# Queries and keys of layer 1's second eight heads by seven products of halves, all sums made by VectorE

## The chip, the cores and the metric

The kernel runs on one core of one Trainium2 chip. The metric is the time of one execution on the device, in microseconds, taken as the median of several runs.

## The reference

An encoder trunk of two layers on 512 tokens of 1024 channels, in float32. Layer 0 mixes tokens by retention, layer 1 by forgetting attention with 16 heads of 64 channels; every layer norms and modulates its input, and adds a gated branch to it. What matters here is the beginning of layer 1's mixer:

```
q, k, v, g, f = split(h @ w_in, [FOX_W, 2 * FOX_W, 3 * FOX_W, 4 * FOX_W])
q = rms_norm(q per head, q_gain) * 64 ** -0.5
k = rms_norm(k per head, k_gain)
logits = q . k + cum[query] - cum[key], causal, in blocks of 128 queries
o = softmax(logits) . v
y = (o * silu(g)) @ w_out
```

Here h is 512 x 1024, and q, k, v and g are 512 x 1024 each.

## The kernel before

**Precision.** A matmul operand is split into a high part in a shorter format and the rest: ScalarE copies (`CAST`), VectorE subtracts (`split`, line 607). Three matmuls then make one product (`mm3`, line 564): high by high, high by low, low by high. A stationary operand has 128 x 128 elements, a moving one 128 x 512.

**Layer 1's projections.** Heads 0 to 7 are group 0, heads 8 to 15 group 1. For a group, `proj1` (line 1697) makes queries, keys and values one after the other, each 512 tokens by 512 channels. Its weights come as four items of 128 x 1024 (two blocks of 128 input channels by 512 outputs): an item is loaded by SyncE into a buffer `raw`, and split into `wh` and `wl`. `proj_b` (line 1073) multiplies: 4 token tiles x 8 blocks of 128 input channels x 3 matmuls, 96 matmuls per projection, into four PSUM banks `p`. `evac_qk` (line 1529) takes queries and keys out: ScalarE copies the bank to `qn` and squares it into `tm`, VectorE sums the squares per head; after the last token tile VectorE makes the reciprocal roots and scales the four tiles. `evac_v1` (line 1551) splits the values into buffers `v`.

**The heads.** For each pair of heads, `stacks` (line 1566) transposes `qn` and splits it into `st`. For each head, `scores` (line 1590) multiplies queries and keys, VectorE adds `ck` (the running sum of the log forget gates, broadcast by SyncE, with the causal mask added by a POOL DMA) and finds the least, ScalarE makes the exponential, POOL scales by the reciprocal sum; `turn` (line 1626) transposes and splits the probabilities into `ph`; `values` (line 1638) multiplies with `v`. `heads` (line 1668) runs the scores of one head beside the turning of the one before.

**Layer 0's products of halves.** `halves` (line 1092) makes two projections of the same input by a scheme with seven products of half size where the plain way has eight. Tokens, input channels and the two outputs are the halves. It needs four sums of the input's quarters (`sums`), sums of weight blocks, and it adds and subtracts products at the end (`put`). A product is 2 token tiles x 4 blocks of 128 channels x 3 matmuls, 24 matmuls, in two halves `kp` with 12 each; each half has its own `wh` and `wl`. The weight sums are made in place in the `raw` buffers: two of them by VectorE (`sum2`), two by DMAs that add in flight on POOL's queue (`plus`). Layer 0 uses it for values and gates of each head, and for half of the output projection.

**Order of the work.** The program is first built as tasks, and then ordered by a planner, `Sched.order` (line 303). A task's priority is TensorE's planned clock when it is emitted plus an offset: weight splits have -6 us (`PROC`), loads -30, what `merge` (line 493) weaves in as side work -1 (`B1`). Each engine takes the ready task with the lowest value whose buffers are free. The order found is fixed then; on the chip each engine runs its own list in that order, and SyncE and POOL issue their DMAs in theirs.

Near line 1709 the main work of layer 1 stands in this order: queries of group 0 (while `norm_b`, line 1414, norms, transposes and splits the tokens), keys of group 0 with the forget gates woven in, values of group 0 with the first stacks and scores, then queries, keys and values of group 1 with heads 0 to 7 (`R1` = 0.5 of side work per unit of main work), then the gates with heads 8 to 15.

**Buffers.** `KINDS` (line 61) gives each kind of buffer its pool and how many of it may live at a time: pool "C" has 60 buffers of 128 x 512 (`N_C`), pool "B" 14 of 128 x 1024 (`N_B`), shared by `raw` (8), `wh` (4), `wl` (4) and `ck` (3). A buffer is free when the last task that uses it is done.

Of the kernel before, what the change touches and what calls it, by code (L numbers as in the profile page):

```python
# [7 lines left out]
F32R = mybir.dt.float32r  # L8
# [51 lines left out]
START, TICK, TICK_COLS = 0.65, 10.24 / 3, 3072  # L60
KINDS = {
# [470 lines left out]
def trunk(tc, x, c, positions, mod_w, mod_b, norm_g, ret_w_in, ret_w_out, fox_w_in, fox_b_f,  # L532
# [6 lines left out]
    with ExitStack() as es:  # L539
# [337 lines left out]
                spread2()  # L877
        extra = [mod_items(1, "g", j) for j in range(2)]
        for g in range(2):
            for nm_, base in (("q", 0), ("k", 1024), ("v", 2048)):  # L880
                add(("f" + nm_, g), w_b(wi1, base + g * 512))
                while g == 0 and nm_ == "k" and extra:
                    spread()
# [205 lines left out]
                        evac(t, banks[t])  # L1089
                    yield 0.648  # L1090

        def halves(key, src, cols, lows, quarter, sums, put, late=False):

# [65 lines left out]
            if not late:  # L1159
                yield from second()  # L1160
            yield from product(v, lambda: sums[1], sum2(first, 2), True)
            third = plus(block(2), c1, lo)
            u5 = keep(v)
            yield from product(x, lambda: sums[2], sum2(first, 3), False)
            fourth = plus(first, c0, lo)
            u2 = keep(x)
            yield from product(v, lambda: sums[4], heads(block(3)), False)
            put(0, 1, v, u2, ALU.subtract)
# [232 lines left out]
        def norm_a(t):  # L1401
# [9 lines left out]
            for nh in range(2):  # L1411
                V.tensor_scalar(out=xns[t][nh], in0=x1[nh], scalar1=r, scalar2=None, op0=ALU.mult)

        def norm_b(t):
            pss = []
            for hf in range(2):
                ps = pr_()
                for k in range(4):
                    T.transpose(ps[:, k * P:(k + 1) * P], xns[t][hf][:, k * P:(k + 1) * P], ident)
                pss.append(ps)  # L1420
            hvs = [s.buf("xn"), s.buf("xn")]
            for k in range(4):
                for hf in range(2):
                    kk = hf * 4 + k
                    a, b = mod_a[:, 1, kk:kk + 1], mod_s[:, 1, kk:kk + 1]
                    ks = slice(k * P, (k + 1) * P)
                    if hf:
                        V.tensor_scalar(out=hvs[hf][:, ks], in0=pss[hf][:, ks], scalar1=a, scalar2=b,
                                        op0=ALU.mult, op1=ALU.add)
                    else:  # L1430
                        A.activation(hvs[hf][:, ks], pss[hf][:, ks], AF.Identity, scale=a, bias=b)
            ts = slice(t * P, (t + 1) * P)
            for hf in range(2):
                split(hvs[hf].rearrange("p (k n) -> p k n", k=4, n=P), h2t[hf][0][:, :, ts],
                      h2t[hf][1][:, :, ts])
# [93 lines left out]
        def evac_qk(name, g):  # L1529
            qn[name, g] = [None] * NT  # L1530
            ss = small(32)

            def f(t, ps):
                raw, sq = qn_(), tm()
                A.copy(raw, ps)
                A.activation(sq, ps, AF.Square)
                V.tensor_reduce(out=ss[:, t * 8:t * 8 + 8],
                                in_=sq.rearrange("p (h d) -> p h d", h=8, d=HD), axis=AX.X, op=ALU.add)
                qn[name, g][t] = raw
                if t == NT - 1:  # L1540
                    r = rsqrt(ss, 32, 1.0 / HD)
                    for tt in range(NT):
                        v = qn[name, g][tt].rearrange("p (h d) -> p h d", h=8, d=HD)
                        rr = r[:, tt * 8:tt * 8 + 8]
                        V.tensor_tensor(out=v, in0=v, in1=rr.unsqueeze(2).to_broadcast([P, 8, HD]),
                                        op=ALU.mult)
            return f

        vt = {}

# [146 lines left out]
        def proj1(names, g, lead=0):  # L1697
            for name in names:
                ev = evac_v1(g) if name == "v" else evac_qk(name, g)
                yield from proj_b(lambda i: W(("f" + name, g), i), h2, ev, lead=lead)  # L1700
# [6 lines left out]
                norm_b(t + 2)  # L1707
        run(q0)
        merge(proj1("k", 0), forget_gates(), 0.5, B1, s)
        merge(proj1("v", 0), chain(stacks(0), stacks(1), scores(0)), 0.3, B1, s)  # L1710
        merge(proj1("qkv", 1), heads(0, 8, 16), R1, B1, s)
        merge(chain(*[proj_g(j) for j in range(4)]), heads(8, 16, 16), R2, B1, s)


# [87 lines left out]
```

## Time and profile before

| what | before |
|---|---|
| median of 3 runs | 717.82 us (715.70 to 718.38) |
| the profiled execution | 717.73 us, span 716.0 us |
| mean granted TensorE clock | 0.996 |
| TensorE busy | 704.0 us, 3388 matmuls |
| VectorE busy | 593.0 us, 1233 instructions |
| ScalarE busy | 409.9 us, 765 instructions |
| GpSimd busy | 119.3 us, 171 instructions |
| bytes moved by DMA | 120.37 MB, of these 111.25 MB read from HBM |

A row of a group names the line, engine and operation, then output <- inputs by the program's buffer names, the shape, the count, and after the bars the busy time in us and the mean of one in ns, and the engine's idle time before it. Nearly every instruction has line 452, where the planned tasks are sent, so groups are told apart by their buffers. A row of the windows has start and end in us from the span's start, the length, the busy time of each engine with its instructions, the granted clock, and the DMA engines' share and rate. PE is TensorE's matmul, PEld its weight load, DVE VectorE, ACT ScalarE, POOL GpSimd, SP SyncE.

### The profile page before, as it was taken

How to read it: one execution, taken by the hardware profiler on the slowest of the kernel's cores; microseconds unless marked ns; L12 is line 12 of the kernel's file. 1: busy time of each engine (PE TensorE's matmuls, PEld its weight loads, DVE VectorE, ACT ScalarE, POOL GpSimd, SP SyncE). 2: the span in 40 equal slices, each digit the busy share in tenths (PEclk: the TensorE clock that was granted, in tenths of full speed). 3: DMA queues.
4: the chain of work that ended last, by engine and by line, in shares of the span. 5: the costliest groups of instructions: out<-in, count | busy, mean ns of one | idle time of the engine just before them, and what ended most of it. 6: DMA issues, size and time to landing. Idle time of an engine off the chain costs nothing.

```text
span 716.0 us, 10129 instructions
## 1 busy us (share of the span) xinstructions
PE 704.0 (98%) x3388; PEld 580.6 (81%) x3388; DVE 593.0 (83%) x1233; ACT 409.9 (57%) x765; POOL 119.3 (17%) x171
## 2 busy tenths in 40 slices
PE   9999999999999999999999999999999999999995
PEld 7877888888888888888888887887888788888884
DVE  4899999989978786999998878886696877789925
ACT  5458664655255525875534553646676667789513
POOL 1001101100110001002000100054334355531011
PEclk9999999999999999999999999999999999999999
DMA  8992864786577635817669217395637465745202
GB/s 283 349 312 76 184 206 131 163 258 217 115 147 234 187 55 130 296 61 148 177 198 300 100 63 264 125 261 130 171 101 172 126 162 143 174 116 178 94 13 106
DMA packets 79636, 120.37 MB, mean 168 GB/s; under 512 B 7016, under 2 KB 39904, under 8 KB 79584
## 3 DMA queue, kind: packets, MB, share of 16 engines
q1 hardware_dynamic: 66176, 98.71, 43.1%
q0 software_dynamic: 13408, 21.01, 17.0%
q8 instruction: 27, 0.44, 0.3%
q14 instruction: 25, 0.20, 0.1%
HBM read 111.25 MB, written 4.25 MB: 161 GB/s over the span
## 4 chain that ended last, share of the span: by engine, by line
PE 90%; DVE 6%; ACT 2%; issue 1%; DMA 0%; DVEq 0%; POOL 0%; ACTq 0%; POOLq 0%
PE p L452 57%; PE r L452 18%; PE a L452 12%; PE s L452 3%; DVE wl L452 1%; DVE sx L452 1%; DVE st L452 1%; ACT lg L452 1%; DVE tg L452 1%; DVE lg L452 0%; DMA crow<-in_c 0%; DVE v L452 0%; ACT st L452 0%; DVE act L452 0%; DVE sf L452 0%
## 5 line engine op out<-in xcount | busy, mean ns | idle before, releaser
L452 DVE TENSOR_TENSOR wl<-raw,wh 128x1024 fp32r<-128x1024 f32 x126 | 153.7, 1225 | 24.3 <-PE p L452 10.5
L452 ACT CAST wh<-raw 128x1024 fp32r<-128x1024 f32 x126 | 131.4, 1053 | 66.0 <-PE p L452 34.7
L452 PE MATMUL p<-wh,big 128*128 128x512 f32 x384 | 135.2, 402 | 0.0
L452 PEld LDWEIGHTS p<-wh,big 128*128 128x128 f32 x384 | 72.1, 188 | 13.4
L452 PE MATMUL p<-wh,sf 128*128 128x512 f32 x256 | 80.7, 392 | 0.0
L452 PE MATMUL p<-wl,big 128*128 128x512 f32 x192 | 76.3, 398 | 0.0
L452 PE MATMUL p<-wh,act 128*128 128x512 f32 x192 | 62.7, 393 | 0.0
L452 POOL DMA_DIRECT2D raw<-in_ret_w_in x16 | 19.4, 1211 | 258.9 <-ACT sf L452 64.2
L452 DVE SCALAR_TENSOR_TENSOR macc<-raw,csilu,macc 128x512 f32<-128x512 f32 x80 | 60.0, 751 | 0.6
L452 PEld LDWEIGHTS p<-wh,sf 128*128 128x128 f32 x256 | 48.0, 188 | 9.6
L452 POOL TENSOR_SCALAR lg<-lg,t 128x512 f32<-128x512 f32 (+1 forms) x64 | 39.3, 660 | 84.5 <-DVE t L452 76.5
L452 PE MATMUL p<-act,wh 128*128 128x512 f32 x160 | 53.3, 393 | 0.0
L452 PE MATMUL p<-wl,sf 128*128 128x512 f32 x128 | 50.2, 392 | 0.0
L452 PE MATMUL p<-big,wh 128*128 128x512 f32 x128 | 46.3, 420 | 0.0
L452 PE MATMUL r<-act,sh 128*128 128x512 f32 x120 | 42.8, 392 | 0.3 <-DVE sh L452 0.3
L452 PEld LDWEIGHTS p<-wh,act 128*128 128x128 f32 x192 | 36.0, 188 | 7.3
L452 ACT ACTIVATE lg<-lg,t 128x512 f32<-128x512 f32 (+1 forms) x64 | 35.9, 563 | 9.2 <-DVE t L452 8.9
L452 PEld LDWEIGHTS p<-wl,big 128*128 128x128 f32 x192 | 36.2, 188 | 6.2
L452 PE MATMUL p<-wh,go 128*128 128x512 f32 x112 | 39.2, 402 | 0.0
L452 PE MATMUL p<-wl,act 128*128 128x512 f32 x96 | 37.9, 394 | 0.5 <-DVE wl L452 0.5
L452 POOL DMA_DIRECT2D ck<-in_k_mask x32 | 28.5, 1029 | 55.0 <-DVE t L452 52.6
L452 DVE TENSOR_TENSOR ph<-r,ph 128x128 fp32r<-128x128 f32 (+2 forms) x64 | 30.8, 484 | 7.0 <-ACT ph L452 6.5
(206 smaller groups left out, 1574.7 us busy)
## 6 DMA issues: line engine op xcount, KB each, us to landing
raw<-in_ret_w_in SPq DMA_DIRECT2D x48, 512.0 KB, 4.9
raw<-in_mod_w SPq DMA_DIRECT2D x64, 256.0 KB, 5.9
raw<-in_fox_w_in SPq DMA_DIRECT2D x32, 512.0 KB, 5.1
raw<-in_ret_w_in POOLq DMA_DIRECT2D x16, 512.0 KB, 6.4
raw<-in_mod_w SPq DMA_DIRECT2D x16, 512.0 KB, 4.6
raw<-in_ret_w_out SPq DMA_DIRECT2D x16, 512.0 KB, 5.1
ck<-cum_dram SPq DMA_DIRECT2D x16, 448.0 KB, 4.4
x<-in_x SPq DMA_DIRECT2D x16, 256.0 KB, 5.9
```

The lines of the kernel that those rows point to most:

```text
L452: getattr(eng, op)(*[real(v) for v in args], **{k: real(v) for k, v in kw.items()})
```

## The change

Queries and keys of group 1 are made by `halves`, in a new generator `queries_keys`, in place of two runs of `proj1`. The two outputs are the 512 columns of the queries and the 512 of the keys. Values of group 1 stay as they are and follow.

- The weights of both come as four blocks of two `raw` buffers, in the order 0, 2, 3, 1, in place of eight items.
- `halves` gets a parameter `moved`. With `moved=False` all four weight sums are made by VectorE in place (`sum2`); no DMA adds.
- The four sums of the input's quarters are made by the new `sums_of_h2`, before the values of group 0 are emitted. It reads the normed tokens in float32, for which `norm_b` keeps its eight buffers `xn` (`hv`), and splits the sums into `sf4` buffers.
- `evac_qk` may get a second operand: VectorE then adds or subtracts it to the bank while writing `qn`, and ScalarE squares `qn` in place of the bank. Two of eight tiles still come as a copy by ScalarE. The roots and scalings of a projection follow when all four token tiles are there.
- `xn` may have 14 buffers in place of 6, `qn` 16 in place of 12; the pools keep their sizes.

```diff
@@ KINDS
-    "sf": ("C", 2), "sh": ("C", 5), "x1": ("C", 10), "xn": ("C", 6), "tm": ("C", 4), "qn": ("C", 12),
+    "sf": ("C", 2), "sh": ("C", 5), "x1": ("C", 10), "xn": ("C", 14), "tm": ("C", 4), "qn": ("C", 16),
@@ the order of the weights
         for g in range(2):
-            for nm_, base in (("q", 0), ("k", 1024), ("v", 2048)):
+            if g == 1:
+                its = w_halves(wi1, 512, 1536, 0, 2)
+                for n in (0, 2, 3, 1):
+                    add(("fqk", n), its[2 * n:2 * n + 2])
+            for nm_, base in (("q", 0), ("k", 1024), ("v", 2048))[2 * g:]:
@@ halves
-        def halves(key, src, cols, lows, quarter, sums, put, late=False):
+        def halves(key, src, cols, lows, quarter, sums, put, late=False, moved=True):
...
-            third = plus(block(2), c1, lo)
+            third = plus(block(2), c1, lo) if moved else sum2(block(2), 3)
...
-            fourth = plus(first, c0, lo)
+            fourth = plus(first, c0, lo) if moved else sum2(first, 1)
@@ after norm_a
+        hv, forms1 = {}, {n: [None] * 4 for n in (1, 2, 3, 4)}
+
+        def sums_of_h2():
+            for kp in range(2):
+                ks, f = slice(2 * kp, 2 * kp + 2), {}
+                for n in (1, 3, 2, 4):
+                    f[n] = s.buf("sx")
+                    for th in range(2):
...
+                        V.tensor_tensor(out=of[n], in0=a, in1=b, op=op)
+                    h, l = s.buf("sf4", 512, F32R), s.buf("sf4", 512, F32R)
+                    split(f[n], h, l)
...
@@ norm_b
+            hv[t] = [v.rearrange("p (k n) -> p k n", k=4, n=P) for v in hvs]
@@ evac_qk
-            def f(t, ps):
+            def f(t, ps, rest=None, op=None):
                 raw, sq = qn_(), tm()
-                A.copy(raw, ps)
-                A.activation(sq, ps, AF.Square)
+                if rest is None:
+                    A.copy(raw, ps)
+                else:
+                    V.tensor_tensor(out=raw, in0=ps, in1=rest, op=op)
+                A.activation(sq, ps if rest is None else raw, AF.Square)
...
-                if t == NT - 1:
+                if all(v is not None for v in qn[name, g]):
@@ new
+        def queries_keys():
+            ev = [evac_qk("q", 1), evac_qk("k", 1)]
+
+            def put(i, j, a, b, op):
+                for tl in range(2):
+                    ev[j](2 * i + tl, a[tl], None if b is None else b[tl], op)
+
+            def half(i, j):
+                c = slice(256 * i, 256 * i + 256)
+                return [(h[:, c], l[:, c]) for h, l in h2[4 * j:4 * j + 4]]
+
+            yield from halves(("fqk",), wi1, (512, 1536), (0, 2), half, forms1, put, True, False)
@@ the order of the work
         merge(proj1("k", 0), forget_gates(), 0.5, B1, s)
+        sums_of_h2()
         merge(proj1("v", 0), chain(stacks(0), stacks(1), scores(0)), 0.3, B1, s)
-        merge(proj1("qkv", 1), heads(0, 8, 16), R1, B1, s)
+        merge(chain(queries_keys(), proj1("v", 1)), heads(0, 8, 16), R1, B1, s)
```

More of the change, by code (lines that the diff above doesn't have):

```diff
@@ L1412, in norm_a @@
                 V.tensor_scalar(out=xns[t][nh], in0=x1[nh], scalar1=r, scalar2=None, op0=ALU.mult)
+        hv, forms1 = {}, {n: [None] * 4 for n in (1, 2, 3, 4)}
[5 more added lines that the diff above has]
+                    for th in range(2):
+                        lo = [hv[th + 2 * i][0][:, ks, :] for i in range(2)]
+                        hi = [hv[th + 2 * i][1][:, ks, :] for i in range(2)]
+                        of = {m: b.rearrange("p (k n) -> p k n", k=2, n=256)[:, :, th * P:(th + 1) * P]
+                              for m, b in f.items()}
+                        a, b, op = {1: (lo[1], hi[1], ALU.subtract), 3: (lo[0], lo[1], ALU.subtract),
+                                    2: (of.get(1), lo[0], ALU.subtract), 4: (hi[0], of.get(2), ALU.add)}[n]
+                        V.tensor_tensor(out=of[n], in0=a, in1=b, op=op)
+                    h, l = s.buf("sf4", 512, F32R), s.buf("sf4", 512, F32R)
+                    split(f[n], h, l)
+                    for j in range(2):
+                        c = slice(256 * j, 256 * j + 256)
+                        forms1[n][2 * kp + j] = (h[:, c], l[:, c])
         def norm_b(t):
```

## The prediction

> **What bounds the kernel now.** First the page: share of the engines, and the chain that ended last.
>
> ```profile
> span 716.0 us, 10129 instructions
> PE 704.0 (98%) x3388; PEld 580.6 (81%) x3388; DVE 593.0 (83%) x1233; ACT 409.9 (57%) x765; POOL 119.3 (17%) x171
> PE 90%; DVE 6%; ACT 2%; issue 1%; DMA 0%; DVEq 0%; POOL 0%; ACTq 0%; POOLq 0%
> ```
>
> TensorE sets the end; VectorE comes next. The execution took 717.73 us, 1.7 us more than its span; the median is 717.82, so a sum against the one is a sum against the other.
>
> Then the windows of the stages that the change touches. I cut them where the p matmuls, counted in 96 per 512-column projection, pass from one projection to the next. The rows after the header are: the keys of group 0; its values; queries and keys of group 1; its values; the gates; and the last four together. Columns: length, then busy time of PE, PEld, DVE, ACT, POOL.
>
> ```profile
> core 0: us, PE busy (x) PEld busy (x) DVE busy (x) ACT busy (x) POOL busy (x), PEclk, DMA share, GB/s
> 436.00:463.75 27.75, 27.75 (x127) 20.97 (x126) 25.58 (x56) 13.20 (x21) 0.00 (x0) 1.00 0.59 200
> 463.75:489.15 25.40, 25.40 (x123) 21.26 (x122) 19.00 (x38) 13.99 (x23) 9.55 (x14) 1.00 0.86 214
> 489.15:556.87 67.72, 67.01 (x354) 55.08 (x353) 49.05 (x128) 46.60 (x113) 27.44 (x45) 1.00 0.57 141
> 556.87:590.77 33.90, 33.78 (x179) 27.57 (x177) 27.21 (x65) 22.43 (x51) 15.49 (x26) 1.00 0.61 152
> 590.77:665.00 74.23, 73.92 (x408) 62.06 (x407) 62.49 (x151) 59.33 (x136) 29.39 (x44) 1.00 0.60 159
> 463.75:665.00 201.25, 200.12 (x1058) 165.97 (x1057) 157.75 (x381) 142.34 (x320) 81.87 (x128) 1.00 0.62 159
> ```
>
> TensorE has about 1 us of idle time in 201. VectorE has 43.5, but only 18.7 of them in the window of the replaced projections. These are what they consist of there:
>
> ```profile
> L452 PE MATMUL p<-wh,big 128*128 128x512 f32 x128 | 50.2, 413 | 0.0
> L452 PE MATMUL p<-wl,big 128*128 128x512 f32 x64 | 25.9, 405 | 0.0
> ...
> L452 DVE TENSOR_TENSOR wl<-raw,wh 128x1024 fp32r<-128x1024 f32 x8 | 9.8, 1228 | 0.7 <-ACT wh L452 0.7
> L452 DVE TENSOR_REDUCE t<-tm 128x8 f32<-128x512 f32 x6 | 4.1, 682 | 3.2 <-ACT tm L452 3.2
> L452 DVE TENSOR_TENSOR qn<-qn,t 128x512 f32<-128x512 f32 x4 | 2.5, 686 | 0.0
> ```
>
> Matmul records overlap, so their mean is no price. The chain has long runs of them:
>
> ```profile
> 203.22 29.39 PE p L452 x129
> 447.01 10.65 PE p L452 x46
> ```
>
> These are 0.228 and 0.232 us each; I use 0.228. The 192 matmuls take 43.8 us, which leaves 23.9 us of the 67.7 to the attention heads woven in.
>
> **TensorE's gain.** Seven products of 24 matmuls replace two projections of 96: 168 for 192, so 24 x 0.228 = **5.5 us less**. The replaced work has 38.3 us left.
>
> **VectorE's price.** What is added does not occur in this stage, but layer 0 has the same operations on the same shapes:
>
> ```profile
> L452 DVE TENSOR_TENSOR raw<-raw,raw x20: 1218/1225/1235, 66.8 to 336.3; 128x1024 f32<-128x1024 f32 x20
> L452 DVE TENSOR_TENSOR sx<-x,x x4: 422/422/423, 49.1 to 65.8; 128x256 f32<-128x256 f32 x4
> L452 DVE TENSOR_TENSOR sf<-sx,sf x8: 684/690/699, 53.3 to 74.0; 128x512 fp32r<-128x512 f32 x8
> L452 DVE TENSOR_TENSOR oa<-p,u x4: 684/688/702, 328.0 to 353.5; 128x512 f32<-128x512 f32 x4
> ...
> 105.50 1.23 DVE L452 TENSOR_TENSOR wl<-raw,wh 128x1024 fp32r<-128x1024 f32 x1
> 106.64 0.16 DVE L452 TENSOR_SCALAR t<-t 128x1 f32<-128x1 f32 x1
> ...
> 112.22 0.70 DVE L452 TENSOR_TENSOR rt<-rt,rt 128x512 f32<-128x512 f32 x1
> 112.82 0.70 DVE L452 TENSOR_TENSOR act<-rt,act 128x512 fp32r<-128x512 f32 x1
> 113.42 0.43 DVE L452 TENSOR_TENSOR sf<-r,dec 128x256 f32<-128x256 f32 x1
> 113.75 0.70 DVE L452 TENSOR_TENSOR act<-rt,act 128x512 fp32r<-128x512 f32 x1
> ```
>
> The last six rows show that a following instruction starts before the last one's record ends: 1.14, 0.60 and 0.33 us from start to start for 1024, 512 and 256 columns. With these:
> - weights: seven products of two blocks are 14 splits where there were 8, 6 more; and four of the products add raw blocks first, 8 sums. 14 x 1.14 = 16.0 us.
> - results: six of eight tiles come out as a sum by VectorE in place of ScalarE's copy, 6 x 0.60 = 3.6 us.
> - `sums_of_h2`: 16 sums of 256 and 8 subtractions of 512 columns, 16 x 0.33 + 8 x 0.60 = 10.1 us.
>
> Together 29.7 us, 19.6 of them inside the products.
>
> **What lies beside.** ScalarE gets 6 casts of 1024 (1.06 us in this stage), 8 of 512 (0.62) and 6 copies `u` for 6 copies `qn`: some 11 us, where it has 32.5 us idle from 463.75 to 556.87 (93.1 less 14.0 and 46.6). Without that cover each cast would stand ahead of a VectorE split. The loads are eight of 512 KB, as before; no DMA accumulates, so POOL's queue, where the masks of the heads stand, gets nothing new. On SP's queue the four loads of group 1's values now wait until the fifth product releases raw buffers. They land 5.1 us after issue, and products six and seven, 11 us of TensorE, lie between; without these the first would be some 5 us late.
>
> ```profile
> L452 ACT CAST wh<-raw 128x1024 fp32r<-128x1024 f32 x8 | 8.5, 1062 | 0.1
> ...
> L452 ACT CAST sf<-sx x8: 603/625/655, 49.5 to 71.7; 128x512 fp32r<-128x512 f32 x8
> ...
> raw<-in_fox_w_in SPq DMA_DIRECT2D x32, 512.0 KB, 5.1
> ```
>
> `sums_of_h2` may run as soon as the normed rows are there, so it can fill VectorE's idle time from 436 to 489: 2.2 + 6.4 = 8.6 us of the 10.1 needed. Bounds: 0, if all of it fits, and 1.5 us, if TensorE waits for the rest. What stands behind these sums is the stacks and scores of the first heads, and TensorE has the values' projection to go on with; I take **0.5**.
>
> **The products.** VectorE's own part of the replaced projections was 8 x 1.14 + 10 x 0.60 + about 1 for small ones = 16.3 us, so the heads took 49.05 - 16.3 = 32.7 us for their 23.9 us of TensorE, 1.37 to 1. Now the products alone want 16.3 + 19.6 = 35.9 us of VectorE for 38.3 us of TensorE. If the stage takes L and VectorE works 0.97 of it, the heads get (0.97 L - 35.9) / 1.37 of TensorE, and TensorE idles L - 38.3 less that. The 0.97 lies between two windows of layer 0, 0.999 and 0.943, where TensorE stayed full:
>
> ```profile
> 60.00:120.00 60.00, 59.47 (x268) 48.95 (x267) 59.92 (x99) 38.77 (x62) 4.90 (x4) 1.00 0.66 172
> 302.00:345.00 43.00, 42.70 (x201) 35.28 (x200) 40.53 (x78) 27.09 (x49) 4.83 (x4) 1.00 0.50 116
> ```
>
> What sets L is the buffers. Of the 14 buffers of 1024 words (`N_B`), eight now hold raw blocks until the fifth product at least, since they go on being summed in place; three go to the heads' `ck`, loaded 30 us of planned time ahead; three are left to `wh` and `wl`, where one pair is in use. A product's half is 12 matmuls, 2.74 us; the next `wh` can stand ready, but its `wl` has no place before the pair is free, and then costs one subtraction and two hand-overs:
>
> ```profile
> 505.69 1.05 ACT L452 CAST wh<-raw 128x1024 fp32r<-128x1024 f32 x1
> 506.77 1.22 DVE L452 TENSOR_TENSOR wl<-raw,wh 128x1024 fp32r<-128x1024 f32 x1 [0.19 <-ACT wh L452]
> ```
>
> At 0.19 each that is 1.6 us, so 14 x 4.35 = 61 us. L = 61 gives the heads 17.0 us and an idle TensorE of 61 - 38.3 - 17.0 = **5.7 us**. The heads' missing 6.9 us of TensorE and 9.5 of VectorE move into values and gates, where VectorE has 108.1 - 89.7 = 18.4 us to spare, so they are not paid twice. Bounds: if a fourth buffer is free, L is about 45 and the idle time 1.0; if VectorE answers 0.6 us late each time, half of one such subtraction, L is 69.5 and the idle time 8.3. I take the middle, as the count of buffers is the program's own.
>
> **Sum:** 717.7 - 5.5 + 5.7 + 0.5 = **718.4 us**, no change; its own range is 717.7 - 5.5 + 1.0 = 713.2 to 717.7 - 5.5 + 8.3 + 1.5 = 722.0.
>
> **Rivals.**
> - *The whole gain stays.* VectorE's work is served in the gaps, as in layer 0, where a window at 0.999 left TensorE 59.47 of 60 busy, with the same kind of products. Over the whole stage, 157.75 + 29.7 = 187.5 us would have to fit into 195.7, a share of 0.958. Against it: the heads wait for VectorE several times each, retention less often. 717.7 - 5.5 = 712.2 to 713.2 us, with the low bounds above.
> - *Slower: VectorE becomes the bound of the whole attention stage.* The heads that are held back don't catch up, because scores, exponentials, transposes and values follow one another through VectorE and it is always behind. Then the stage lasts 187.5 us over the share that VectorE reaches. The busiest stretch of heads now is this one, 0.906:
>
> ```profile
> 626.00:660.00 34.00, 34.00 (x188) 28.46 (x187) 30.79 (x71) 30.01 (x67) 9.92 (x15) 1.00 0.48 133
> ```
>
>   187.5 / 0.906 = 207.0 us, 5.8 more than 201.2: 723.5 us. It decides below a share of 187.5 / 201.2 = 0.932, where the gain is used up. Against it: in that stretch TensorE was full, so the share is no proven ceiling.
> - *The clock.* If the idle time comes in a few long gaps, TensorE's clock falls. The last 8 us show it, with TensorE busy for 0.66:
>
> ```profile
> 708.00:716.00 8.00, 0.66 (x6) 0.46 (x4) 3.22 (x12) 1.74 (x5) 0.74 (x1) 0.83 0.35 132
> ```
>
>   0.17 x 8 = 1.4 us of full clock lost for one gap. Three gaps while products wait, at the first, third and fifth, make 718.4 + 4.2 = 722.6 us. Against it: gaps of 1.6 us into which heads fall are short, and every window of the stage has 1.00. The Trainium skill, "TensorE: Matmul & The Clock Gate", Part 1, says that the clock halves after an idle window of about 3.4 us; the row at the end agrees in kind. By that rule, waits of 1.6 us cost no clock and the sum stays as it is.
>
> That the change doesn't do what it says I leave out: the 24 matmuls are gone by the program.
>
> **Chances.** No change 0.38, the whole gain 0.26, VectorE the bound 0.30, the clock 0.06. A measurement of this kernel can tell about 0.5%, 3.6 us, from no change; faster ends at 714.2 and slower begins at 721.4. The first case's own range reaches a little past both bounds, and I leave it whole: faster 0.26, same 0.38, slower 0.36. The range reaches from the whole gain, 712.3, to somewhat past the slower case, 726: its price goes by one share, and at 0.895 it would be 187.5 / 0.895 = 209.5, 8.3 over, which is 726.0.
>
> **What would show it.** TensorE with 24 matmuls fewer, 3364. VectorE some 30 us busier in all, with 28 more long `TENSOR_TENSOR`s of 1024 or 512 columns in the splits. Right: 5 to 6 us of TensorE idle between 489 and 556, ended by `wl`, in pieces below 2 us; heads later by some 7 us at the end of the products and caught up by 665. The buffers: a `wl` subtraction that starts when the pair before it is done, not earlier. Wrong: no idle there (first rival); idle before `ph`, `st` or `lg` during values and gates (second); a window with a clock below 1.00 (third). If `sums_of_h2` holds up the first scores by more than 2 us, the 0.5 was too small.

## The result, and the profile after

| | before | after |
|---|---|---|
| median of 6 runs each, on the same chip | 717.86 us (715.70 to 718.68) | 722.16 us (721.06 to 725.61) |
| ratio after to before | | 1.0077, 95% interval 1.0054 to 1.0100 |
| the profiled execution | 717.73 us, span 716.0 us | 725.29 us, span 723.5 us |

The change makes the kernel slower, by 0.77%. This ratio is taken over all runs of both kernels; the two medians alone give 1.0060. The time lies within the range on record, but the likeliest case, no change, did not come; "slower" had been given 0.36. The profiled execution of the change took 725.29 us and the median is 722.16, so up to 3 us of what its profile shows are not in the median.

The first lines of the page of the changed kernel:

```profile
span 723.5 us, 10170 instructions
PE 703.6 (97%) x3364; PEld 576.6 (80%) x3364; DVE 620.6 (86%) x1277; ACT 421.1 (58%) x779; POOL 127.7 (18%) x171
```

TensorE has its 24 matmuls fewer. VectorE is 27.6 us busier, ScalarE 11.2. GpSimd is 8.4 us busier with the same 171 instructions: its scalings take longer (the last section has them), which the prediction had nowhere.

The windows of the same stages, cut at the same matmuls as before (keys of group 0, its values, the products, values of group 1, gates, and the last four together):

```profile
core 0: us, PE busy (x) PEld busy (x) DVE busy (x) ACT busy (x) POOL busy (x), PEclk, DMA share, GB/s
463.98:489.22 25.24, 25.02 (x117) 20.01 (x116) 19.36 (x36) 11.54 (x20) 9.50 (x14) 1.00 0.89 211
489.22:559.85 70.63, 62.96 (x316) 50.15 (x314) 61.28 (x137) 53.30 (x111) 29.54 (x40) 0.98 0.47 118
559.85:597.80 37.95, 37.21 (x199) 29.63 (x197) 33.43 (x83) 25.02 (x61) 20.32 (x28) 1.00 0.59 145
597.80:672.70 74.90, 74.68 (x408) 62.33 (x407) 64.19 (x152) 59.56 (x138) 30.90 (x47) 1.00 0.64 162
463.98:672.70 208.72, 199.87 (x1034) 162.11 (x1033) 178.25 (x404) 149.42 (x326) 90.27 (x128) 0.99 0.60 150
```

The products' stage did not become shorter by 5.5 us. It became 2.9 us longer, 70.63 for 67.72, with 7.67 us of idle TensorE where there had been 0.71. The values of group 1 took 4.05 us more, 37.95 for 33.90, mostly since heads that were put off are done there: 199 matmuls stand in that window for 179. The gates are unchanged within 0.7 us.

Now what ended TensorE's idle time. First the four groups of its matmuls from 463.98 to 672.7 that had most of it (two more had 0.3 and 0.2 us), then the two groups that had any before, from 463.75 to 665 (the last columns: idle time before them, and its releasers):

```profile
L452 PE MATMUL p<-wl,big 128*128 128x512 f32 x88 | 35.3, 401 | 0.4 <-DVE wl L452 0.4
L452 PE MATMUL r<-st,st 128*128 128x512 f32 (+3 forms) x128 | 33.9, 335 | 0.6 <-DVE st L452 0.4
L452 PE MATMUL r<-ident,lg 128*128 128x128 f32 x160 | 31.3, 283 | 6.9 <-POOL lg L452 6.4 <-DVE st L452 0.3
L452 PE MATMUL p<-wl,sf 128*128 128x512 f32 x32 | 13.3, 416 | 0.5 <-DVE wl L452 0.5
```

```profile
L452 PE MATMUL r<-ident,lg 128*128 128x128 f32 x160 | 31.4, 274 | 0.4 <-POOL lg L452 0.3
L452 PE MATMUL r<-ph,v 128*128 128x512 f32 (+3 forms) x128 | 30.2, 323 | 0.7 <-ACT ph L452 0.7
```

Not the weight halves `wl`, but the transposes of the probabilities `lg` had TensorE waiting: 6.9 us for 0.4. They wait for POOL's scaling. Three rows of TensorE's timeline show the two largest pieces (the time in brackets is the engine's idle time before the row):

```profile
508.20 0.40 PE L452 MATMUL p<-wh,sf 128*128 128x512 f32 x1
511.65 0.90 PE L452 MATMUL r<-ident,lg 128*128 128x128 f32 x3 [3.05 <-POOL lg L452]
...
538.66 0.55 PE L452 MATMUL r<-ident,lg 128*128 128x128 f32 x3 [1.75 <-POOL lg L452]
```

And what POOL did meanwhile, in its timeline:

```profile
496.88 3.97 POOL L452 TENSOR_SCALAR lg<-lg,t 128x512 f32<-128x512 f32 x4 [15.10 <-DVE t L452]
500.80 1.80 POOL L452 DMA_DIRECT2D ck<-in_k_mask  x2
503.36 2.14 POOL L452 TENSOR_SCALAR lg<-lg,t 128x512 f32<-128x512 f32 x2 [0.76 <-DVE t L452]
509.30 1.78 POOL L452 DMA_DIRECT2D ck<-in_k_mask  x2 [3.80 <-PE p L452]
510.55 1.38 POOL L452 TENSOR_SCALAR lg<-lg,t 128x256 f32<-128x256 f32 x2
```

Before, all four scalings of a head stood ahead of the two mask DMAs, for every head of this stage. The first head's rows:

```profile
489.54 2.05 POOL L452 TENSOR_SCALAR lg<-lg,t 128x512 f32<-128x512 f32 x4 [8.10 <-DVE t L452]
491.55 1.74 POOL L452 DMA_DIRECT2D ck<-in_k_mask  x2
```

The timeline of SyncE's queue in the changed kernel has the two loads of `ck` for these masks, the second issued at 502.73 (494.38 + 8.69 less the 0.34 of one issue):

```profile
494.38 8.69 SPq L452 DMA_DIRECT2D ck<-cum_dram  x2
```

The view of the DMA issues around 502.73 has the time from issue to landing of that one load, its last column:

```profile
ck<-cum_dram SPq DMA_DIRECT2D x1, 448.0 KB, 5.7
```

A head has four scalings. In the change, two of the second head's are done at 505.5; then, in POOL's fixed order, stand the two DMAs that add the mask to the next head's `ck`, and only then the other two scalings. The load of that `ck` was issued at 502.73 and landed 5.7 us later, at about 508.4. (The row of the mask DMAs names a matmul as the last releaser; the same row in experiment 5 names the load.) So the mask DMAs waited, the two scalings behind them waited, the transposes waited, and TensorE, which is in order too, stood still for 3.05 us. VectorE stood still as well, and so had no lack of time there:

```profile
512.91 0.29 DVE L452 CUSTOM_DVE_ANT_0 lg<-r,ck 128x128 f32<-128x128 f32 x1 [3.73 <-PE r L452]
```

The same order came again before the second piece, with two mask DMAs between two scalings and the next. The load of their `ck` was issued at 530.43 and landed 4.1 us later:

```profile
530.31 1.26 POOL L452 TENSOR_SCALAR lg<-lg,t 128x512 f32<-128x512 f32 x2 [3.61 <-DVE t L452]
535.18 1.85 POOL L452 DMA_DIRECT2D ck<-in_k_mask  x2 [3.60 <-DVE t L452]
536.37 3.78 POOL L452 TENSOR_SCALAR lg<-lg,t 128x256 f32<-128x256 f32 x4
```

After the first gap TensorE's clock fell, as the window around it shows:

```profile
511.00:515.00 4.00, 3.35 (x14) 3.10 (x15) 1.99 (x5) 1.62 (x5) 1.23 (x4) 0.57 0.72 164
```

0.43 x 4 = 1.7 us of full clock. 3.05 + 1.75 + 1.7 = 6.5 us of the profiled execution hang on this order of POOL's, the 1.75 also on the slow scalings behind the masks, 3.78 us for four (experiment 5).

### The profile page after: what moved, and what is told of

Same layout as the page of the kernel before. It is cut to its first block, busy times and chain, and to the rows that moved or that the text cites. A ratio compares the mean times of both kernels' runs of the same rounds, so it can differ in the third digit from the quotient of the medians.

```text
span 723.5 us, 10170 instructions
## 1 busy us (share of the span) xinstructions
PE 703.6 (97%) x3364; PEld 576.6 (80%) x3364; DVE 620.6 (86%) x1277; ACT 421.1 (58%) x779; POOL 127.7 (18%) x171
## 5 line engine op out<-in xcount | busy, mean ns | idle before, releaser
L452 DVE TENSOR_TENSOR wl<-raw,wh 128x1024 fp32r<-128x1024 f32 x132 | 160.5, 1221 | 21.9 <-PE p L452 11.8
L452 PE MATMUL p<-wh,sf 128*128 128x512 f32 x320 | 105.0, 397 | 0.0
L452 PE MATMUL p<-wh,big 128*128 128x512 f32 x304 | 104.2, 400 | 0.0
L452 PEld LDWEIGHTS p<-wh,sf 128*128 128x128 f32 x320 | 60.3, 189 | 11.3
L452 PEld LDWEIGHTS p<-wh,big 128*128 128x128 f32 x304 | 56.9, 188 | 11.3
L452 PE MATMUL p<-wl,sf 128*128 128x512 f32 x160 | 63.6, 397 | 0.5 <-DVE wl L452 0.5
L452 POOL TENSOR_SCALAR lg<-lg,t 128x512 f32<-128x512 f32 (+1 forms) x64 | 49.0, 851 | 74.3 <-DVE t L452 67.5
L452 PE MATMUL p<-wl,big 128*128 128x512 f32 x152 | 60.5, 398 | 0.4 <-DVE wl L452 0.4
L452 PE MATMUL r<-ident,lg 128*128 128x128 f32 x160 | 31.3, 283 | 6.9 <-POOL lg L452 6.4
L452 PEld LDWEIGHTS p<-wl,sf 128*128 128x128 f32 x160 | 30.2, 189 | 6.5 <-DVE wl L452 1.0
```

The lines of the kernel that those rows point to most:

```text
L452: getattr(eng, op)(*[real(v) for v in args], **{k: real(v) for k, v in kw.items()})
```

## A measure for all kernels

Idle time is only part of it: a clock of one half and small delays between matmuls are no idle time in the profile. So for each kernel I also summed the start-to-start intervals of its matmuls over the three stages (products, values, gates), less what the same matmuls take when nothing waits, by the intervals in these traces: 0.226 us for 512 columns, 0.173 for 384, 0.120 for 256, 0.110 for 128, 0.109 for a transpose. That sum without waits is 169.8 us for the kernel before, 165.4 with the seven products, and 170.8 in the experiment that puts off a few scores only. What is left is called **waiting** here.

| kernel | ratio to before (95%) | products, values, gates (us) | waiting (us) |
|---|---|---|---|
| before | 1 | 67.7, 33.9, 74.2 | 6.0 |
| the change | 1.0077 (1.0054 to 1.0100) | 70.6, 38.0, 74.7 | 17.9 |
| 1 masks behind | 1.0084 (1.0060 to 1.0109) | 65.2, 39.4, 75.2 | 14.4 |
| 2 no weight sums | 1.0008 (0.9994 to 1.0022) | 63.6, 37.6, 74.7 | 10.5 |
| 3 moved sums | 1.0191 (1.0161 to 1.0220) | 72.1, 43.5, 74.8 | 25.0 |
| 4 input sums alone | 1.0026 (1.0001 to 1.0050) | 67.9, 33.9, 74.1 | 5.1 |
| 5 reduce for sum | 1.0084 (1.0064 to 1.0104) | 69.7, 38.0, 74.7 | 17.0 |
| 6 one more buffer | 0.9992 (0.9978 to 1.0006) | 64.4, 38.0, 74.9 | 11.9 |
| 7 scaling on ScalarE | 1.0052 (1.0035 to 1.0070) | 64.7, 41.2, 74.7 | 15.2 |
| 8 the same, before | 1.0012 (0.9984 to 1.0040) | 68.5, 34.7, 74.6 | 8.0 |
| 9 before, one more buffer | 0.9971 (0.9957 to 0.9985) | 67.7, 33.9, 74.3 | 6.3 |
| 10 experiments 1 and 6 | 1.0031 (1.0012 to 1.0050) | 64.5, 39.6, 75.2 | 14.0 |
| 11 two more buffers | 0.9979 (0.9965 to 0.9994) | 64.1, 37.4, 74.8 | 10.8 |
| 12 one more buffer, less side work | 1.0028 (1.0008 to 1.0048) | 63.6, 35.3, 79.9 | 13.3 |

The ratios are over all timed runs, against runs of the kernel before on the same chip. The stages and the waiting are of the one profiled execution, which can be some us from the median: 725.29 for 722.16 us in the change, 720.55 for 722.72 in 1, 733.25 for 729.75 in 3, 727.66 for 720.67 in 7, 723.99 for 718.42 in 12. The experiments ran in three groups (1 to 4, 5 to 8, 9 to 12), each on a chip of its own, so I compare ratios, not times.

The change's waiting grew by 11.9 us. The products' saving in this measure is 4.4 us in the three stages, and 1.1 in the values of group 0, where 4 score matmuls stand for 10. So the 5.5 us were saved in full, and in the profiled execution waiting took more than twice as much.

## The experiments

**1. The mask adds behind.** If POOL's order is the cause, the mask DMAs need only come later in the plan: -6 us in place of the loads' -30.

```diff
             with s.at(-30.0):
                 SY.dma_start(ck, cum_dram[head].partition_broadcast(P))
+            with s.at(-6.0):
                 G.dma_start(ck[:, 2 * P:3 * P], k_mask[:, 0:P], accum_op=ALU.add)
                 G.dma_start(ck[:, 4 * P:7 * P], k_mask, accum_op=ALU.add)
```

> The changed kernel, but the two POOL DMAs that add the causal mask to a head's ck get a planned priority 24 us later, so that in POOL's order they stand behind the scalings of the head before. Buffers and VectorE's work stay as they are. If POOL's queue is the cause (mask adds wait for late ck loads, the scalings behind them hold TensorE's transposes), the gaps of 3.05 and 1.75 us go, and the half-clock stretch with them: 722.2 - 4.8 = 717.4 us or a little less. If the buffers of the weights or VectorE's share are the cause, as the prediction had it, the time stays at 721 to 723. If the slow scalings beside VectorE are the cause, it stays within 1 us, too.

Median 722.72 us, ratio 1.0084. Two rows of POOL's timeline:

```profile
501.93 2.94 POOL L452 TENSOR_SCALAR lg<-lg,t 128x512 f32<-128x512 f32 x4 [0.76 <-DVE t L452]
508.01 1.78 POOL L452 DMA_DIRECT2D ck<-in_k_mask  x2 [3.14 <-PE r L452]
```

And two groups of TensorE's matmuls, from 455 to 680:

```profile
L452 PE MATMUL r<-st,st 128*128 128x512 f32 (+3 forms) x128 | 33.9, 338 | 1.8 <-DVE ph L452 1.2 <-DVE oT L452 0.2
L452 PE MATMUL r<-ident,lg 128*128 128x128 f32 x160 | 30.1, 276 | 1.9 <-POOL lg L452 1.7
```

The four scalings of the head now stand ahead of the mask DMAs, and the gap is gone: 1.9 us before the transposes, no lowered clock. The products' stage is 5.4 us shorter. But the values' stage is 1.4 longer, the scores now wait 1.8 us, and the time over all runs is no better than the change's. The profile is of 720.55 us, 2.2 below the median, so part of what this kernel loses is not in it. POOL's order explains the gap; that it explains the loss of time is not shown.

**2. The change without its weight sums.** The eight sums of raw blocks are left out; queries and keys of group 1 are then not the reference's.

```diff
-                    V.tensor_tensor(out=raw[i], in0=raw[i], in1=block(n)[i], op=ALU.add)
+                    if moved:
+                        V.tensor_tensor(out=raw[i], in0=raw[i], in1=block(n)[i], op=ALU.add)
+                    else:
+                        block(n)
```

> The changed kernel without the eight sums of raw weight blocks in the new products (queries and keys of group 1 are thus made from unsummed blocks); loads, splits and matmuls stay. VectorE has 8 x 1.14 = 9.1 us less. If VectorE's share is what costs, most of the idle time goes: 717 us. If the buffers are, each wl still waits for its pair: 720 to 722. If POOL's queue is, the late ck load stays and so does the gap: 721. If scalings are slowed by VectorE instructions with two SBUF inputs, their mean falls from 851 ns to some 750, and 1 to 2 us go.

Median 717.58 us, ratio 1.0008: with 8 x 1.14 = 9.1 us of VectorE out of the chain, 0.69% or 5.0 us come back. The products' window:

```profile
487.67:551.31 63.64, 60.96 (x315) 48.75 (x314) 55.43 (x131) 52.16 (x110) 25.73 (x40) 1.00 0.52 131
```

TensorE does the same 315 to 316 matmuls in 7.0 us less, and the clock stays at 1.00. But even so the saving does not appear: waiting is 10.5 us for 6.0 before.

More than VectorE's time changed here. With eight instructions fewer the planner found another order, and POOL's timeline has all four scalings of the second head ahead of the masks:

```profile
498.58 2.05 POOL L452 TENSOR_SCALAR lg<-lg,t 128x512 f32<-128x512 f32 x4 [0.81 <-DVE t L452]
505.16 1.78 POOL L452 DMA_DIRECT2D ck<-in_k_mask  x2 [4.54 <-DMA ck<-cum_dram]
```

The masks wait 4.54 us for their load, longer than in the change, and cost TensorE nothing. So the 5.0 us cannot be put down to VectorE's time alone.

**3. Two of the four sums moved.** The other form of `halves`: two weight sums come by DMAs on POOL's queue that add in flight.

```diff
-            yield from halves(("fqk",), wi1, (512, 1536), (0, 2), half, forms1, put, True, False)
+            yield from halves(("fqk",), wi1, (512, 1536), (0, 2), half, forms1, put, True)
```

> The changed kernel with two of the four weight sums made by DMAs that add in flight (POOL's queue), as in layer 0: four VectorE sums fewer, 4.6 us, and four POOL DMAs more, 1.2 us each to issue. If VectorE's share is the cause: 719 to 720. If POOL's queue is: more things that wait stand ahead of the scalings, 723 to 727.

Median 729.75 us, ratio 1.0191. VectorE has less to do and the kernel is slower still. The beginning of POOL's timeline in the products:

```profile
493.95 1.22 POOL L452 DMA_DIRECT2D raw<-in_fox_w_in  x1 [8.14 <-DVE t L452]
497.32 3.97 POOL L452 TENSOR_SCALAR lg<-lg,t 128x512 f32<-128x512 f32 x4 [2.15 <-DVE t L452]
```

And two groups of TensorE's matmuls, from 455 to 680:

```profile
L452 PE MATMUL r<-ph,v 128*128 128x512 f32 (+3 forms) x128 | 29.9, 335 | 3.4 <-DVE ph L452 3.1
L452 PE MATMUL p<-wl,sf 128*128 128x512 f32 x32 | 13.6, 426 | 3.3 <-DVE wl L452 3.3
```

The adding loads stand in POOL's queue between scalings and masks, and now `wl` is late, by 3.3 us. So less work for VectorE is no gain in itself; it matters what stands in the queues in its place.

**4. The input sums alone.** `sums_of_h2` and the buffers `xn` that it needs are put into the kernel before; nothing uses them.

```diff
-    "sf": ("C", 2), "sh": ("C", 5), "x1": ("C", 10), "xn": ("C", 6), "tm": ("C", 4), "qn": ("C", 12),
+    "sf": ("C", 2), "sh": ("C", 5), "x1": ("C", 10), "xn": ("C", 14), "tm": ("C", 4), "qn": ("C", 12),
...
+        sums_of_h2()
```

> The kernel before with the four sums of the input's quarters made and split as in the change, but read by nothing; queries and keys stay plain projections. It prices that part: 10.1 us of VectorE and 24 buffers. Prediction: 0.5 us, 717.9 + 0.5 = 718.4. If the later first scores (492.6 for 485.5 in the changed kernel) come from it and cost, up to 2 us more.

Median 717.98 us, ratio 1.0026, at the edge of nothing. VectorE is busy for 601.5 us, 8.5 more; the span is 716.0 us, as before. Six score matmuls are put off into the next stage, as in the change, and the stages from there on are as before. The 10 us of sums are hidden.

**5. A reduction for each sum.** On POOL, four scalings of the first head took 3.97 us in the change, where VectorE's splits and sums, with two operands from SBUF each, run beside them. Before, the same four took 2.05. To see if this is the cost, each of the eight sums becomes a `TENSOR_REDUCE` of the same length with one operand; queries and keys of group 1 are then not the reference's.

```diff
-                    V.tensor_tensor(out=raw[i], in0=raw[i], in1=block(n)[i], op=ALU.add)
+                    if moved:
+                        V.tensor_tensor(out=raw[i], in0=raw[i], in1=block(n)[i], op=ALU.add)
+                    else:
+                        block(n)
+                        V.tensor_reduce(out=raw[i][:, 0:8], in_=raw[i].rearrange("p (h d) -> p h d", h=8, d=P),
+                                        axis=AX.X, op=ALU.add)
```

> The changed kernel with each of the eight sums of raw weight blocks replaced by a VectorE instruction that takes about as long and stands at the same place in the same chain, but reads one SBUF operand: a TENSOR_REDUCE over the 1024 columns of the block into 8 of its own columns (queries and keys of group 1 are thus not the reference's). If VectorE's time is what costs, the time stays with the changed kernel's, 721 to 723. If it is that POOL's scalings stand still while VectorE reads two SBUF operands, the time goes to that without sums, 717 to 718.5, the slow scalings become fewer, and the transposes' waits for them fall from 9.7 us of excess to some 3.

Median 722.90 us, ratio 1.0084: the same as the change. Rows of POOL's timeline:

```profile
495.20 3.02 POOL L452 TENSOR_SCALAR lg<-lg,t 128x512 f32<-128x512 f32 x4 [13.89 <-DVE t L452]
498.16 1.79 POOL L452 DMA_DIRECT2D ck<-in_k_mask  x2
501.27 1.25 POOL L452 TENSOR_SCALAR lg<-lg,t 128x512 f32<-128x512 f32 x2 [1.32 <-DVE t L452]
507.69 1.78 POOL L452 DMA_DIRECT2D ck<-in_k_mask  x2 [5.17 <-DMA ck<-cum_dram]
508.94 1.38 POOL L452 TENSOR_SCALAR lg<-lg,t 128x256 f32<-128x256 f32 x2
```

And the window around the gap:

```profile
506.00:514.00 8.00, 4.46 (x20) 3.66 (x19) 3.67 (x11) 4.20 (x10) 3.54 (x6) 0.79 0.50 122
```

POOL's scalings are quicker, 1.25 us for two in place of 2.14. POOL then only waits longer, 5.17 us for 3.80, for the same mask DMAs, and here the row itself names what they wait for: the load of `ck`. The gap and the lowered clock come again. At the place of the change's second piece POOL has the same order and a wait of 3.01 us, but its next two scalings take 1.52 us, and TensorE's timeline shows no idle time there. So the slower scalings have a part in the second piece, but they make neither the first gap nor the time over all runs.

**6. One more buffer.** If the shortage of buffers of 1024 words sets the order and the lateness, one more must mend it. Two of 512 words pay for it.

```diff
-N_C, N_B = 60, 14
+N_C, N_B = 58, 15
```

> The changed kernel with 15 buffers of 1024 words and 58 of 512 in place of 14 and 60, the same memory. A fourth buffer is then free for wh and wl while eight raw blocks are held. By the prediction's step on the buffers, TensorE's idle time in the products falls from 5.7 to 1.0 us: 717 to 718. If the waits are for POOL's scalings, as the profile has it (9.7 us of excess before transposes, 1.1 before wl), less than 1.5 us change: 721 to 723; the loads of ck may come earlier, which would take away the gap of 3 us.

Median 715.68 us, ratio 0.9992: 0.85% or 6.1 us come back, with all of the change's work in place. Rows of POOL's timeline:

```profile
502.74 2.88 POOL L452 TENSOR_SCALAR lg<-lg,t 128x512 f32<-128x512 f32 x4 [0.62 <-PE p L452]
508.86 1.78 POOL L452 DMA_DIRECT2D ck<-in_k_mask  x2 [3.24 <-PE r L452]
```

The products' window:

```profile
487.87:552.29 64.42, 61.41 (x315) 49.00 (x314) 61.46 (x137) 51.54 (x110) 31.43 (x41) 1.00 0.53 129
```

And the group of the transposes, from 455 to 680:

```profile
L452 PE MATMUL r<-ident,lg 128*128 128x128 f32 x160 | 30.5, 276 | 2.4 <-POOL lg L452 1.4 <-DVE st L452 1.0
```

The order that the planner finds with 15 buffers has all four scalings of that head ahead of the mask DMAs. These still wait, 3.24 us, since their load is not earlier (issued at 503.91, for 502.73 in the change), but nothing that TensorE needs stands behind them. A later head has its masks between two scalings and two here too, with a wait of 2.75 us, and TensorE's timeline shows no idle time there. Waiting falls by 6.0 us, about as much as the two gaps and the clock had cost (6.5). VectorE is as busy as in the change, 61.46 us in a stage 6.2 us shorter, a share of 0.954 for 0.868.

**7 and 8. Scaling on ScalarE.** The scalings of heads 0 to 7 leave POOL's queue, in the change (7) and, as a control, in the kernel before (8).

```diff
-                        G.tensor_scalar(out=lg[j], in0=lg[j], scalar1=rs[:, j:j + 1], scalar2=1.0,
-                                        op0=ALU.mult, op1=ALU.mult)
+                        if head < 8:
+                            A.activation(lg[j], lg[j], AF.Copy, scale=rs[:, j:j + 1])
+                        else:
+                            G.tensor_scalar(out=lg[j], in0=lg[j], scalar1=rs[:, j:j + 1], scalar2=1.0,
+                                            op0=ALU.mult, op1=ALU.mult)
```

> The changed kernel with the scaling of the probabilities of heads 0 to 7 made by ScalarE (activation Copy with a scale per partition) in place of POOL; the same result. The transposes then wait for neither POOL's queue nor its slow stretches, but ScalarE gets four instructions per head more, some 2.2 us each head, in a stage where it is 75% busy. If POOL (queue or slowness) is the cause: 717 to 719. If VectorE's share is: 722 or more.

> The kernel before with the same move of the scalings of heads 0 to 7 to ScalarE, as a control. There the transposes had 1.4 us of excess waiting for scalings in the window of the products. Expected 716.5 to 718.5, no change; if it is faster by 3 us or more, the move is worth it without the change, and e7 shows nothing of the change.

Medians 720.67 and 718.31 us, ratios 1.0052 and 1.0012. The products' stage of the change falls to 64.7 us, so the gap goes here too, but the values' stage rises to 41.2. The control has 2.0 us more of waiting itself. Of the 6.0 us that the products gain, the values lose 3.2. The two ratios of the change, 1.0077 and 1.0052, have overlapping intervals, so no gain in time is shown.

**9. The kernel before with one more buffer.** The control for 6: the same line in the kernel before.

```diff
-N_C, N_B = 60, 14
+N_C, N_B = 58, 15
```

> The kernel before with 15 buffers of 1024 words and 58 of 512, the control to e6. If the buffer helps the new products only, this stays at 716.5 (715.5 to 717.5), and e6's gain of 6.5 us over the changed kernel belongs to the stage of the products. If it helps layer 0's weights as well, this is 1 to 1.5 us faster than before, by as much as e6's layer 0 was shorter, and the change with more buffers is no better than the kernel before with them.

Median 714.78 us, ratio 0.9971, the quickest kernel of all. Its stages in layer 1 are as before, to 0.2 us, and waiting is 6.3; the window of queries and keys of group 1:

```profile
485.27:553.01 67.74, 67.03 (x354) 54.90 (x353) 49.18 (x128) 46.63 (x113) 27.52 (x45) 1.00 0.57 142
```

The gain lies ahead of them, in layer 0: the first matmul of layer 1's queries comes at 407.7 us in place of 411.6 in the profiled executions. Not all of these 3.9 us are the buffer's. Near the start the clock was lowered in the profiled execution of the kernel before, and not in this one. Their windows there, the kernel before first:

```profile
15.00:32.00 17.00, 17.00 (x94) 15.16 (x94) 14.46 (x27) 8.74 (x13) 0.00 (x0) 0.90 1.10 349
15.00:32.00 17.00, 17.00 (x100) 14.57 (x99) 15.41 (x25) 8.03 (x11) 0.00 (x0) 1.00 1.10 349
```

That is 0.10 x 17 = 1.7 us of full clock. The 2.2 us that are left agree with the ratio, 0.29% or 2.1 us. So of the 6.1 us of experiment 6, about 2 are no repair of the change, and about 4 are.

**10. Experiments 1 and 6 together.** Both edits, the mask adds at -6 and one more buffer.

```diff
-N_C, N_B = 60, 14
+N_C, N_B = 58, 15
...
+            with s.at(-6.0):
```

> e6 with the mask adds put behind the scalings in POOL's planned order, as in e1. In e6 two mask adds already came to stand behind four scalings. If POOL's order is what e6 mended, this adds nothing: 715 to 716.5. If both count by themselves, 1 to 2 us less, 714.

Median 719.63 us, ratio 1.0031: worse than one more buffer alone. In its profile the values' stage is longer, 39.6 us for 38.0, as in experiment 1, where the masks stand as late; that they hold the heads back there is likely, but not shown.

**11. Two more buffers.**

```diff
-N_C, N_B = 60, 14
+N_C, N_B = 56, 16
```

> The changed kernel with 16 buffers of 1024 words and 56 of 512. If the places of wh and wl are the bound, a fifth place saves a further 1 to 2 us in the products; if one buffer was enough, it is e6's 715.7, and the four smaller buffers taken from the heads cost up to 2 us: 715 to 718.

Median 715.03 us, ratio 0.9979. Against 0.9971 for the kernel before with one more, the seven products still bring nothing: waiting is 10.8 us, 4.5 more than there, and the intervals of the two ratios overlap. The kernel before with two more buffers was not tried.

**12. One more buffer, and less side work.** If the heads ask for more than VectorE and POOL can give beside the products, weaving in less must help: `R1` from 0.50 to 0.44, beside the line of experiment 6.

```diff
-R0, R1, R2, R3 = 0.45, 0.5, 0.84, 0.35
+R0, R1, R2, R3 = 0.45, 0.44, 0.84, 0.35
```

> e6 with R1 = 0.44 in place of 0.5: fewer head steps woven into the products and the values, more left to the gates. VectorE's demand in the products falls by some 12% of the heads' share, about 3 us, and the waits of transposes for scalings there (4.4 us of excess in e6) should fall by 1 to 2. If VectorE's share in the products is what is left: 714 to 715. If the heads left over pile up at the gates: 716 to 718.

Median 718.42 us, ratio 1.0028: worse than experiment 6. The products and the values become 0.8 and 2.7 us shorter, but the gates 5.0 us longer: their window has 438 matmuls for 408, since heads are put off into it.

## Why the prediction was right or wrong

- **TensorE's gain, 5.5 us: right.** 24 matmuls fewer, and by the counted intervals all 5.5 us were saved.
- **VectorE's and ScalarE's added work, 29.7 and 11 us: right** in size, 27.6 and 11.2. (The terms of VectorE's own part in the old products add up to 16.1 us, not 16.3, which changes nothing.)
- **`sums_of_h2`, 0.5 us: nearly right.** With these sums alone (4) the span did not move, and the ratio, 1.0026, is hardly clear of 1.
- **The heads put off: too much.** I gave the heads 17.0 of 23.9 us, 29% put off; 146 of 161 of their matmuls were done in the products' stage, 9% put off. They were caught up in the values, as forecast: 100 matmuls of theirs for 79 there, and as many as before in the gates.
- **The buffers as the cause: right that their count matters, wrong in the path.** This is the step that failed. I had the shortage act through `wl` having no place, in pieces below 2 us. The idle time before `wl` was 0.9 us in all, and 6.4 us stood before the transposes, behind POOL's scalings. I wrote that POOL's queue "gets nothing new". It got no new instruction, but another order: two scalings stood behind mask DMAs that waited for a late load of `ck`. One more buffer (6) gives back 6.1 us, some 4 of them beyond what it gives the kernel before (9), and with it the four scalings stand ahead of the masks. But the load of `ck` came no earlier there, so what makes it late is not shown. And with that order mended by itself (1), the gap went and the time over all runs stayed. So POOL's order is shown as the cause of the gap, and only argued as the cause of the 4 us: with 15 buffers the whole plan is another one.
- **The idle time, 5.7 us: too small.** 7.67 us of idle time, with the clock and the small delays 10.0 us more waiting in the products, and 1.9 in values and gates. The upper bound, L of 69.5 us with 8.3 of idle time, is near what came, 70.6 with 7.67, but by luck: it stood for a VectorE that is late before `wl`, and what came was a wait for POOL before the transposes.
- **L = 61 us and a share of 0.97: both wrong.** The stage took 70.6 us at a share of 0.868. Without the gaps (6) it took 64.4 at 0.954, nearer to both.
- **The rival with VectorE as the bound: its price came near, its reason did not come.** It had 723.5 us, and the median is 722.16. It was to decide at a share below 0.932 of the whole stage; the share was 178.25 / 208.72 = 0.854, but VectorE stood still in the largest gap, so it was not what held TensorE there. Its work may count all the same: without the eight sums (2) 5.0 us come back, although a reduction as long in their place (5) gives nothing. So the two operands of the sums are not what costs. Whether the sums cost by delaying the heads or by giving the planner another order, these runs don't separate, as in 2 both change together.
- **The rival with the clock: it happened, once, in place of three times,** and for 1.7 us as I had priced one gap at 1.4. The Trainium skill, "TensorE: Matmul & The Clock Gate", Part 1, has the clock halve after an idle window of about 3.4 us. Here a gap of 3.05 us was enough: in the 3.41 us before the clock fell, TensorE worked for 0.60. Experiment 3 shows that less is enough, and that waits of 1.6 us can cost clock: there it worked for 1.58 us, its longest gap was 1.57 us, and the next 3.41 us had one half of the clock:

```profile
525.72:529.13 3.41, 1.58 (x9) 1.10 (x9) 3.07 (x12) 2.76 (x9) 0.68 (x2) 1.00 0.26 100
529.14:532.55 3.41, 3.41 (x11) 2.84 (x10) 1.16 (x3) 0.63 (x1) 1.58 (x5) 0.50 0.42 135
```

  A gap of 2.13 us in the same run, ended at 564.78, and the 1.75 us in the change had no lowered clock behind them. So the length of one gap does not decide.
- **My signs** showed the forecast to be wrong: one piece of 3.05 us, and a window at 0.98. They did not name the case that came: idle time ended by `lg` was to show the second rival, in values and gates, and it came in the products.

What stays open is the second half of the loss. In 2 and 6, without the gap of 3 us, 4.5 and 5.9 us of waiting more than before remain, about what the seven products save; in 11, 4.8 remain, of which 1.5 are a piece before the transposes again. In 1, 7, 10 and 12 more remains, 7.3 to 9.2 us. In 6 the largest part is before the transposes, 4.4 us in the products for 1.4 before, by the same count. 15 buffers without the weight sums, and the change in a fixed order with only one thing varied, were not tried.

## What to carry to other kernels

A change that holds buffers longer is priced by following what is late next, through every in-order queue: here a load, the mask DMA that waits for it on GpSimd, the scalings behind that DMA, the transposes behind those. An engine that has idle time is no cover as such: at a share of 0.87 VectorE stood still in the largest gap, and what has to be asked is whether the added work stands ahead of something on the path. Where a planner orders the program, every edit also changes the order, so an experiment's profile has to be read for the order before its time is put down to the edit. When more of a resource mends a change, give the same resource to the kernel before: with one more buffer that kernel is the quickest of all, and the change with one or two more buffers brings no gain over it.

## What the runs showed of the hardware

- **POOL's scaling slows beside VectorE.** The mean of its 64 scalings rose from 660 ns to 851, by the page's group before and then after:

```profile
L452 POOL TENSOR_SCALAR lg<-lg,t 128x512 f32<-128x512 f32 (+1 forms) x64 | 39.3, 660 | 84.5 <-DVE t L452 76.5
```

```profile
L452 POOL TENSOR_SCALAR lg<-lg,t 128x512 f32<-128x512 f32 (+1 forms) x64 | 49.0, 851 | 74.3 <-DVE t L452 67.5
```

  Counted by overlap (of a quarter of a us or more), a scaling with a VectorE instruction of two SBUF operands beside it took 1.4 us on average in the kernel before (7 of them) and 1.7 in the change (15); with none beside it some 0.6 us in both; beside a reduction with one operand (5) 0.56 us. The Trainium skill, "GPSIMD Engine Reference", 1. Specifications, says that GpSimd shares its SBUF interfaces with VectorE, with contention from instructions with two SBUF inputs; the trace agrees, and gives the size.
- **The clock's periods.** The lowered clock of 0.5 in the change lasted 3.41 us, from 511.4 to 514.8, right after the gap, by the trace's record of the clock. Experiments 3 and 5 have a stretch of the same length behind a gap. Apart from these and from the end of each kernel, where the record shows 0.5 again, there is only a stretch near the start, beginning between 15 and 18 us. It lasted 3.41 us in the profiled executions of the kernel before, the change, 3, 4, 6, 8, 10 and 11, four times as long, 13.65 us, in 7 and 12, and did not occur in 1, 2, 5 and 9. With TensorE full, as it was there in the kernel before (17.00 of 17.00 us busy in the window under experiment 9), the short one costs 1.7 us and the long one 6.8, which no edit made. What brings it about is not shown.
